# Transfers begun on GpSimd's queue in a two-layer recurrent decoder step on one core

## The chip, the core and the metric

The kernel runs on one core of a Trainium2 chip. The time is that of one execution on the device, in microseconds; "before" is the median of three runs, 2912.96 us (2909.19 to 2916.35). One more execution was profiled; its times are those of the rows below.

## The reference, cut to what matters

One inference step of a trunk of two layers is computed for 256 prompt tokens (one sequence) and 8 samples of 4 tokens each, in float32, with 2048 features. The same weights serve both groups.

```python
# layer 0: one projection feeds gated DeltaNet (8 heads, 128x128 state) and RG-LRU (width 1024)
proj = x @ w_in_e                                    # conv inputs, z, gate, a_pre, b_pre
conv_out, conv_new = causal_conv(conv_in, conv_buf, w_conv, b_conv)      # width 4
g, beta = -exp(a_log) * softplus(a_pre + dt_bias), sigmoid(b_pre)
o, s_new = gated_delta_rule(q, k, v, g, beta, s_delta)   # S = exp(g) S (I - beta k k^T) + beta k v^T
h, h_last = rg_lru(xr, r_pre, i_pre, lam, h_lru)         # h = a h + sqrt(1 - a^2) (i x)
mix = concat([rms_norm(o) * silu(z), h * gelu(gate)]) @ w_out_e
# layer 1: mLSTM, 8 heads, dk 128, dv 256, running-max stabiliser
h, c, n, m = mlstm_chunked(q, k, v, ig, fg, c0, n0, m0)
mix = (rms_norm(h) * sigmoid(o_pre)) @ w_out_o
# every layer
h = layer_norm(alpha * x + mix)
h = layer_norm(alpha * h + square(relu(h @ w_up)) @ w_down)
x = h + sigmoid(h @ w_ple_gate) * (p[layer] @ w_ple)
```

The outputs are y for both groups and all new states: the last three inputs of the convolutions, the DeltaNet, LRU and mLSTM states.

## The kernel before, in words

All 288 tokens (256 + 32) lie along the free dimension, features along the partitions. Each weight matrix is cut into slabs of 128x8x128 float32, 512 KB each. A slab is loaded into `raw` (line 394) and split into two float32r parts: ScalarE writes `hi`, a rounded copy (line 294), VectorE writes `lo = raw - hi` (line 295). The activations are split in the same way (`ah`/`al` and `bh`/`bl`), and each 128x128x288 product is three matmuls, hi*hi, lo*hi and hi*lo (line 416), 24 a slab. `raw` has four buffers, and three slabs are kept ahead in the two mixers (six elsewhere).

The kernel runs load, mixer of layer 0, output projection, LayerNorm, MLP, LayerNorm, gate, and then the same for layer 1. In a mixer the heads' work is written as generators, which `tick` advances by one step after every twelve slab matmuls, so that the small matmuls of the heads stand between those of the projection. TensorE works strictly in the order thus laid down, as does every other engine and every queue; the order of each is chosen ahead of time by the framework (Tile), which also places all semaphores. It may put an instruction that needs nothing earlier ahead of others: the state loads of line 1010 stand on SyncE's queue long before the heads that use them.

What moves by DMA, by place in the code:

- `load`: x, parameters, constants, first slabs (SyncE).
- `conv` (lines 672 and 676), 32 times: the samples' earlier inputs into `cin`, the new ones out of it. `cin` has two buffers. ScalarE copies the projection into the rest of `cin` in between.
- `delta_gates` (lines 703 to 727): a row of resets comes in, the cumulated log decays `gc` go out to DRAM (`dgc`), and three small arrays go out (`dds`) and come back with the samples' rows on the partitions (`rs`). These are begun on ScalarE's queue.
- `delta_head` (line 857): `gcb`, one head's row of `dgc`, comes back broadcast over 128 partitions. GpSimd copies the samples' parts of k, q, v, z and `gcb` (lines 861 to 863). Line 935 stores the prompt's state.
- `delta_sample`: 16 loads of four samples' states, 256 KB each, in four buffers (line 1010), each followed by two GpSimd copies into a window `win` (line 1019) and eight small matmuls that read the state itself; then 16 loads again, an update on VectorE and a store (line 1074).
- `lru_block` (line 1111): the two 128x128 gate weights `wri`.
- `mlstm_gates` (lines 1219 to 1268): as in layer 0, with `dng`, `mds`, `mrs`, `dw`, `w` and `scB`; begun on ScalarE's queue.
- `mlstm_head`: `ngb` (line 1304), the prompt's new state (line 1380), the samples' states `cn`, 514 KB each, in three buffers (line 1394) and their stores (line 1413).
- `scratch` (line 527): the layer's `p`. `gate`: the output y.

Of the kernel before, what the change touches and what calls it, by code (L numbers as in the profile page):

```python
# [16 lines left out]
NP, NS = 256, 32  # L17
NT = NP + NS
# [200 lines left out]
class Trunk:  # L219
# [299 lines left out]
    def scratch(self, layer):  # L519
        sm = self.sm  # L520
        T = lambda n, s, d=F32: sm.tile([128, *s], d, name=n, bufs=1)
        self.Y, self.Z = T("Y", [16, NT]), T("Z", [16, NT])
        self.s1, self.s2 = T("s1", [NT]), T("s2", [NT])
        self.mu, self.var, self.rstd, self.lnw = T("mu", [NT]), T("var", [NT]), T("rstd", [NT]), T("lnw", [NT])
        self.php = T("ph", [2, NT], F32R), T("pl", [2, NT], F32R)
        raw = T("praw", [2, NT])
        self.nc.sync.dma_start(raw, self.t["p"][layer])
        self.split(*self.php, raw)
        self.layer = layer
        self.extra = self.ex  # L530
        self.cap = 6
# [135 lines left out]
    def conv(self, lp, acc, c):  # L667
        nc, p = self.nc, self.p
        w = lambda j: p[:, P_WCONV + 4 * c + j:P_WCONV + 4 * c + j + 1]
        x = self.cin[self.ncin % len(self.cin)]  # L670
        self.ncin += 1
        nc.sync.dma_start(x[:, S0:], self.t["sconv"][c])
        nc.scalar.copy(x[:, 3:S0], acc[:, :NP])
        nc.scalar.copy(x[:, S0:].rearrange("p (b t) -> p b t", t=7)[:, :, 3:7],
                       acc[:, NP:].rearrange("p (b t) -> p b t", t=4))
        nc.sync.dma_start(self.t["conv"][c], x[:, NP:])
        out = lp.tile([128, S0 + 56], F32, name="cv")
        o = out[:, :NW]
        self.act(o, x[:, 3:3 + NW], AF.Identity, bias=p[:, P_BCONV + c:P_BCONV + c + 1], scale=w(3))
        for j in range(3):  # L680
            self.stt(o, x[:, j:j + NW], w(j), o, ALU.mult, ALU.add)
        return out
# [14 lines left out]
    def delta_gates(self, acc, lp, T):  # L697
        nc, p, c = self.nc, self.p, self.c
        acc = yield from self.gate_rows(acc, T)
        rg = T(40)  # L700
        nc.vector.memset(rg, 0.0)
        x, sp, g, rst = T(), T(), T(), T()
        nc.scalar.dma_start(rst, self.t["rows"][:, 0])
        self.act(x, acc[0:8], AF.Identity, bias=p[0:8, P_DT:P_DT + 1])
        be = rg[32:40]
        self.act(be, acc[32:40], AF.Tanh, scale=0.5)
        self.ts(be, be, 1.0, ALU.add, 0.5, ALU.mult)
        l = self.log1p_exp_neg_abs(x, T)
        self.ts(sp, x, 0.0, ALU.max)
        self.stt(sp, l, 2.0, sp, ALU.mult, ALU.add)  # L710
        ea = lp.tile([8, 1], F32, name="ea")
        self.act(ea, p[0:8, P_AL:P_AL + 1], AF.Exp)
        self.ts(g, sp, ea, ALU.mult, -1.0, ALU.mult)
        gc = rg[0:8]
        nc.vector.tensor_tensor_scan(out=gc, data0=rst, data1=g, initial=0.0, op0=ALU.mult, op1=ALU.add)
        self.dgc = self.dr.tile([8, NT], F32, name="dgc")
        nc.scalar.dma_start(self.dgc, gc)

        gl = T()[:, :NS].rearrange("h (b t) -> h b t", t=4)
        gs = gc[:, NP:].rearrange("h (b t) -> h b t", t=4)  # L720
        nc.vector.tensor_copy(gl, gs[:, :, 3:4].to_broadcast([8, 8, 4]))
        ds = self.dr.tile([3, 8, 8, 4], F32, name="dds")
        for n, r in enumerate((gs, be[:, NP:].rearrange("h (b t) -> h b t", t=4), gl)):
            nc.scalar.dma_start(ds[n].rearrange("b h t -> h b t"), r)
        self.rs = lp.tile([128, 3, 2], F32, name="rs")
        for n in range(3):
            nc.scalar.dma_start(self.rs[:, n], ds[n].rearrange("(g b) h t -> (b h t) g", g=2))

        for _ in range(LATE):
            yield  # L730
        tp = self.pm([128, 2, 40])
        for ch in range(2):
            self.tr(tp[:, ch], rg[:, ch * 128:(ch + 1) * 128])
        tg = lp.tile([128, 2, 40], F32, name="tg")
        nc.vector.tensor_copy(tg, tp)
        gT, self.bT = tg[:, :, 0:8], tg[:, :, 32:40]
        K = lambda n: lp.tile([128, 2, 8], F32, name=n)
        self.ngT, self.egT, self.negT, self.wT, self.eglB = K("ngT"), K("egT"), K("negT"), K("wT"), K("eglB")
        self.ts(self.ngT, gT, -1.0, ALU.mult)
        self.act(self.egT, gT, AF.Exp)  # L740
        self.ts(self.negT, self.egT, -1.0, ALU.mult)
        yield
        pl = self.pm([128, 2, 8])
        self.mm(pl, c[:, C_LAST:C_LAST + 128], gT)
        self.act(self.eglB, pl, AF.Exp)
        self.tt(self.wT, pl, gT, ALU.subtract)
        self.act(self.wT, self.wT, AF.Exp)
# [105 lines left out]
    def delta_head(self, lp, h, kq, v, z, out):  # L853
        nc = self.nc
        yield
        gcb = lp.tile([128, NT], F32, name="gcb")
        nc.sync.dma_start(gcb, self.dgc[h:h + 1].to_broadcast([128, NT]))
        cp = nc.gpsimd.tensor_copy
        gs, zsm = (a[:, NP:].rearrange("p (b t) -> p b t", t=4) for a in (gcb, z))
        for i, s in enumerate((kq[:, 0], kq[:, 1], v)):  # L860
# [71 lines left out]
        self.mm(p2[:, 1], ksc[:, 1], y[:, 1])  # L932
        self.tt(o[:, 1], o[:, 1], p2[:, 0], ALU.add)
        self.stt(S[:, 1], S[:, 0], self.eglB[:, 1, h:h + 1], p2[:, 1], ALU.mult, ALU.add)
        nc.sync.dma_start(self.t["delta_p"][h], S[:, 1])
        self.sumsq(lp, mo[:, 1:2], o[:, 1])
        f = self.delta_f(lp, ssq, mo)
        for ch in range(2):
# [17 lines left out]
    def delta_sample(self, lp, win, out):  # L956
# [50 lines left out]

        def load(h, g):
            s = lp.tile([128, 4, 128], F32, name="S", bufs=4)
            nc.sync.dma_start(s, state(h, g))  # L1010
            return s

        for g in range(2):
# [39 lines left out]
        for g in range(2):  # L1053
# [11 lines left out]
            for h in range(8):  # L1065
                s = load(h, g)
                pu = self.pm([128, 4, 128])
                self.mm(pu, kh, y4)
                if h < 7:
                    kh = keys(h + 1)  # L1070
                for b in range(4):
                    self.stt(s[:, b], s[:, b], self.eglS[:, h, 4 * g + b:4 * g + b + 1], pu[:, b],
                             ALU.mult, ALU.add)
                nc.sync.dma_start(self.t["delta_s"][h, :, 4 * g:4 * g + 4], s)
                yield

    def lru_consts(self, lp):
# [29 lines left out]
    def lru_block(self, lp, n, xr, gates, out):  # L1107
        nc, p = self.nc, self.p
        T = lambda nm, w=NW, **k: lp.tile([128, S0 + 56], F32, name=nm, **k)[:, :w]
        w = lp.tile([128, 2, 128], F32, name="wri")  # L1110
        nc.sync.dma_start(w, self.t["wri"][n])
        for _ in range(2):
            yield
        x = xr[:, :NW]
# [39 lines left out]
    def layer0_mixer(self, x, n_out):  # L1154
        nc, tc, t = self.nc, self.tc, self.t
        with ExitStack() as ctx:
# [47 lines left out]
                gates[n] = self.gelu(lr, next(accs))  # L1204
            self.finish(heads)
            self.finish()
            nc.sync.dma_start(t["lru"], self.hl)
        return out


    def mlstm_gates(self, acc, lp, T):
# [4 lines left out]
        rm = T(72)  # L1216
        nc.vector.memset(rm, 0.0)
        ig, fg, ls, B, d1, g, m, rst, rmx, ng = (T() for _ in range(10))
        nc.scalar.dma_start(rst, self.t["rows"][:, 1])
        nc.scalar.dma_start(rmx, self.t["rows"][:, 2])  # L1220
        self.act(ig, acc[0:8], AF.Identity, bias=p[0:8, P_IG:P_IG + 1])
        nc.vector.tensor_copy(fg, acc[32:40])
        self.ts(fg, fg, p[0:8, P_FG:P_FG + 1], ALU.add)
# [14 lines left out]
        mo = lp.tile([8, 9], F32, name="mout")  # L1238
        nc.vector.tensor_copy(mo[:, 0:1], m[:, NP - 1:NP])
        nc.vector.tensor_copy(mo[:, 1:9], b4(m)[:, :, 3])  # L1240
        nc.scalar.dma_start(self.t["mm"], mo)
        self.ts(ng, g, -1.0, ALU.mult)
        self.dng = self.dr.tile([8, NT], F32, name="dng")
        nc.scalar.dma_start(self.dng, ng)

        mg, nm, wr = (bt(T()[:, :NS]) for _ in range(3))
        sc = T()[:, :8]
# [3 lines left out]
        self.tt(sc, m0, b4(g)[:, :, 3], ALU.subtract)  # L1251
        ds = self.dr.tile([3, 8, 8, 4], F32, name="mds")
        for n, r in enumerate((b4(a), mg, nm)):
            nc.scalar.dma_start(ds[n].rearrange("b h t -> h b t"), r)
        self.rs = lp.tile([128, 3, 2], F32, name="mrs")
        for n in range(3):
            nc.scalar.dma_start(self.rs[:, n], ds[n].rearrange("(g b) h t -> (b h t) g", g=2))
        dw = self.dr.tile([8, 8, 4], F32, name="dw")
        nc.scalar.dma_start(dw, wr)
        self.w4 = lp.tile([128, 8], F32, name="w4")  # L1260
        for q in range(4):
            nc.scalar.dma_start(self.w4[32 * q:32 * q + 32], dw.rearrange("h b t -> (b t) h"))
        self.act(self.w4, self.w4, AF.Exp)
        self.ts(self.w4, self.w4, DKS, ALU.mult)
        dsc = self.dr.tile([8, 8], F32, name="dsc")
        nc.scalar.dma_start(dsc, sc)
        self.scB = lp.tile([128, 8, 8], F32, name="scB")
        nc.scalar.dma_start(self.scB, dsc[None].to_broadcast([128, 8, 8]))
        self.act(self.scB, self.scB, AF.Exp)

        for _ in range(LATE):
# [29 lines left out]
    def mlstm_head(self, lp, h, kq, v, win):  # L1301
        nc, c = self.nc, self.c
        ngb = lp.tile([128, NT], F32, name="ngb", bufs=1)
        nc.sync.dma_start(ngb, self.dng[h:h + 1].to_broadcast([128, NT]))
        smp = lambda a: a[:, NP:].rearrange("p (b t) -> p b t", t=4)
        cp = nc.gpsimd.tensor_copy
        wn = win[h % 2]
# [69 lines left out]
            self.mm(pc, ksc[:, ch], vt[:, ch, 0:257], ch == 0, ch == 1)  # L1377
        so = lp.tile([128, 257], F32, name="cs", bufs=1)
        nc.scalar.copy(so, pc)
        nc.sync.dma_start(self.t["mc_p"][h], so)  # L1380
        yield
        pt = self.pm([128, 2, 2, 128])
        for i in range(2):
# [6 lines left out]
        for g in range(2):  # L1390
            yield
            cn = lp.tile([128, 4, 257], F32, name="cn", bufs=3)
            gs = slice(4 * g, 4 * g + 4)
            nc.sync.dma_start(cn, self.t["smlstm"][h, :, gs])
            pin = self.pm([128, 257])
            for b in range(4):
                self.mm(pin[32 * b:32 * b + 32], wn[:, 4 * g + b, 28 - 4 * h:60 - 4 * h], cn[:, b])
# [8 lines left out]
            for b in range(4):  # L1406
                if b % 2 == 0:
# [2 lines left out]
                self.mm(pu, k8[:, b], v2)  # L1410
                self.stt(cn[:, b], cn[:, b], self.scB[:, h, 4 * g + b:4 * g + b + 1], pu[:, 0:257],
                         ALU.mult, ALU.add)
            nc.sync.dma_start(self.t["mc_s"][h, :, gs], cn)

    def mlstm_sample(self, lp):
        nc, c = self.nc, self.c
# [135 lines left out]
```

## Time and profile before

| | |
|---|---|
| median of three runs | 2912.96 us |
| profiled execution | 2916.8 us, its span 2915.0 us |
| TensorE matmuls | 2888.7 us busy, 99% of the span |
| VectorE, ScalarE, GpSimd | 1732.1, 1318.7, 57.9 us busy |
| granted TensorE clock | 0.999 of full speed over the span |
| DMA | 487.15 MB, 167 GB/s |

Busy time is that of an engine's own instructions; issuing a transfer is shown as an instruction of a queue (SPq is SyncE's, ACTq ScalarE's) and not counted as busy. In a timeline the brackets give the engine's idle time before an instruction and what ended it. The chain of waits is followed back from the last instruction, from each piece to what released it.

### The profile page before, as it was taken

How to read it: one execution, taken by the hardware profiler on the slowest of the kernel's cores; microseconds unless marked ns; L12 is line 12 of the kernel's file. 1: busy time of each engine (PE TensorE's matmuls, PEld its weight loads, DVE VectorE, ACT ScalarE, POOL GpSimd, SP SyncE). 2: the span in 40 equal slices, each digit the busy share in tenths (PEclk: the TensorE clock that was granted, in tenths of full speed). 3: DMA queues.
4: the chain of work that ended last, by engine and by line, in shares of the span. 5: the costliest groups of instructions: out<-in, count | busy, mean ns of one | idle time of the engine just before them, and what ended most of it. 6: DMA issues, size and time to landing. Idle time of an engine off the chain costs nothing.

```text
span 2915.0 us, 52851 instructions
## 1 busy us (share of the span) xinstructions
PE 2888.7 (99%) x21728; PEld 2839.1 (97%) x21728; DVE 1732.1 (59%) x2872; ACT 1318.7 (45%) x2171; POOL 57.9 (2%) x197
## 2 busy tenths in 40 slices
PE   8999999999999999999999999999999999999999
PEld 7999889999999999999999999999999999999999
DVE  7787787754454454455766666567445445445574
ACT  5555676543343343443634444436334334334362
POOL 1000100000000000000000000000000000000000
PEclk9999999999999999999999999999999999999999
DMA  6444475455555555555446665554555554555543
GB/s 225 134 127 128 151 233 174 134 191 166 167 164 164 165 167 166 162 165 166 159 157 201 198 201 172 184 167 159 166 163 163 167 167 162 165 166 166 165 156 132
DMA packets 155298, 487.15 MB, mean 167 GB/s; under 512 B 28552, under 2 KB 35888, under 8 KB 155056
## 3 DMA queue, kind: packets, MB, share of 16 engines
q1 hardware_dynamic: 151632, 483.68, 51.6%
q8 instruction: 170, 2.79, 0.4%
q10 hardware_dynamic: 3424, 0.10, 0.1%
q14 instruction: 72, 0.59, 0.1%
HBM read 466.12 MB, written 17.58 MB: 166 GB/s over the span
## 4 chain that ended last, share of the span: by engine, by line
PE 91%; DVE 5%; ACT 2%; DMA 1%; issue 1%; SPq 0%; ACTq 0%; DVEq 0%
PE acc L416 86%; PE m L268 4%; DVE Y L255 1%; DVE lo L295 1%; PE m L272 1%; ACT hi L294 1%; ACT junk L265 0%; PE m L470 0%; ACT L265 0%; DMA bh<-in_x 0%; DVE cv L258 0%; DVE al L255 0%; DVE mq L258 0%; DVE bl L255 0%; DMA S<-in_sdelta 0%
## 5 line engine op out<-in xcount | busy, mean ns | idle before, releaser
L295 DVE TENSOR_TENSOR lo<-raw,hi 128x1024 fp32r<-128x1024 f32 (+1 forms) x841 | 1027.1, 1223 | 680.6 <-ACT hi L294 679.6
L294 ACT CAST hi<-raw 128x1024 fp32r<-128x1024 f32 (+1 forms) x841 | 880.1, 1048 | 1007.3 <-PE acc L416 708.4
L416 PE MATMUL acc<-ah,hi 128*128 128x288 f32 x3328 | 998.9, 301 | 6.7 <-ACT hi L294 4.9
L416 PE MATMUL acc<-bh,hi 128*128 128x288 f32 x3328 | 989.6, 298 | 0.0
L416 PE MATMUL acc<-ah,lo 128*128 128x288 f32 x3328 | 985.1, 296 | 0.2 <-DVE lo L295 0.2
L416 PE MATMUL acc<-al,hi 128*128 128x288 f32 x3328 | 982.0, 297 | 0.9 <-DVE al L295 0.5
L416 PE MATMUL acc<-bh,lo 128*128 128x288 f32 x3328 | 981.3, 295 | 0.0
L416 PE MATMUL acc<-bl,hi 128*128 128x288 f32 x3328 | 974.1, 294 | 0.6 <-DVE bl L255 0.3
L416 PEld LDWEIGHTS acc<-ah,hi 128*128 128x128 f32 x3328 | 627.1, 189 | 12.6 <-ACT hi L294 4.9
L416 PEld LDWEIGHTS acc<-bh,hi 128*128 128x128 f32 x3328 | 624.0, 188 | 7.7 <-issue 7.1
L416 PEld LDWEIGHTS acc<-ah,lo 128*128 128x128 f32 x3328 | 627.7, 189 | 3.7 <-issue 2.3
L416 PEld LDWEIGHTS acc<-al,hi 128*128 128x128 f32 x3328 | 627.3, 189 | 3.6 <-issue 1.4
L416 PEld LDWEIGHTS acc<-bl,hi 128*128 128x128 f32 x3328 | 624.9, 188 | 1.8 <-DVE bl L255 0.8
L416 PEld LDWEIGHTS acc<-bh,lo 128*128 128x128 f32 x3328 | 625.2, 188 | 0.4
L265 ACT ACTIVATE tmp<-acc 128x288 f32<-128x288 f32 x160 | 65.8, 411 | 307.8 <-PE acc L416 307.7
L255 DVE TENSOR_TENSOR tmp<-tmp 128x288 f32<-128x288 f32 x128 | 58.8, 459 | 155.0 <-ACT tmp L265 155.0
L258 DVE SCALAR_TENSOR_TENSOR Y<-Y,acc 128x288 f32<-128x288 f32 x128 | 58.2, 455 | 112.0 <-PE acc L416 112.0
L258 DVE SCALAR_TENSOR_TENSOR cv<-cin,params,cv 128x312 f32<-128x312 f32 x96 | 51.5, 536 | 0.5
L258 DVE SCALAR_TENSOR_TENSOR cn<-cn,scB,m 128x257 f32<-128x257 f32 x64 | 27.9, 478 | 18.9 <-PE m L268 18.9
L265 ACT ACTIVATE Y<-Y,params 128x288 f32<-128x288 f32 x64 | 37.5, 633 | 0.3
L294 ACT CAST bh<-tmp 128x288 fp32r<-128x288 f32 x80 | 34.7, 434 | 6.2 <-DVE tmp L258 4.4
L258 DVE SCALAR_TENSOR_TENSOR tmp<-tmp,Z 128x288 f32<-128x288 f32 x32 | 14.6, 457 | 38.3 <-ACT tmp L265 38.3
(386 smaller groups left out, 1554.0 us busy)
## 6 DMA issues: line engine op xcount, KB each, us to landing
raw<-in_w_up SPq DMA_DIRECT2D x256, 512.0 KB
raw<-in_w_down SPq DMA_DIRECT2D x256, 512.0 KB
raw<-in_w_in_o SPq DMA_DIRECT2D x96, 512.0 KB
raw<-in_w_in_e SPq DMA_DIRECT2D x95, 512.0 KB
raw<-in_w_gate SPq DMA_DIRECT2D x64, 512.0 KB
raw<-in_w_out_e SPq DMA_DIRECT2D x32, 512.0 KB
raw<-in_w_out_o SPq DMA_DIRECT2D x32, 512.0 KB
cn<-in_smlstm SPq DMA_DIRECT2D x16, 514.0 KB
```

Source lines behind the costliest of these rows:

```text
L255: return self.nc.vector.tensor_tensor(out=out, in0=a, in1=b, op=op)
L258: self.nc.vector.scalar_tensor_tensor(out=out, in0=a, scalar=s, in1=b, op0=op0, op1=op1)
L265: return self.nc.scalar.activation(out, a, f, **k)
L268: self.nc.tensor.matmul(out, l, r, start=start, stop=stop)
L272: self.nc.tensor.transpose(out, a, self.ident[:n, :n])
L294: self.nc.scalar.copy(hi, src)
L295: self.nc.vector.tensor_sub(lo, src, hi.bitcast(F32))
L416: self.nc.tensor.matmul(acc, l[:, k], x[r](8 * kb + k), start=at == 0, stop=at == n - 1)
```

## The change

All transfers but the weight slabs, x, parameters, constants, and the last output y are begun on GpSimd's queue (`nc.gpsimd.dma_start`) instead of SyncE's (`nc.sync`) and ScalarE's (`nc.scalar`). Sources, destinations, buffers and the places in the program text stay as they are. Cut to one place of each kind:

```diff
-        self.nc.sync.dma_start(raw, self.t["p"][layer])
+        self.nc.gpsimd.dma_start(raw, self.t["p"][layer])
...
-        nc.sync.dma_start(x[:, S0:], self.t["sconv"][c])
+        nc.gpsimd.dma_start(x[:, S0:], self.t["sconv"][c])
...
-        nc.sync.dma_start(self.t["conv"][c], x[:, NP:])
+        nc.gpsimd.dma_start(self.t["conv"][c], x[:, NP:])
...
-        nc.scalar.dma_start(self.dgc, gc)
+        nc.gpsimd.dma_start(self.dgc, gc)
...
-            nc.scalar.dma_start(ds[n].rearrange("b h t -> h b t"), r)
+            nc.gpsimd.dma_start(ds[n].rearrange("b h t -> h b t"), r)
...
-            nc.scalar.dma_start(self.rs[:, n], ds[n].rearrange("(g b) h t -> (b h t) g", g=2))
+            nc.gpsimd.dma_start(self.rs[:, n], ds[n].rearrange("(g b) h t -> (b h t) g", g=2))
...
-        nc.sync.dma_start(gcb, self.dgc[h:h + 1].to_broadcast([128, NT]))
+        nc.gpsimd.dma_start(gcb, self.dgc[h:h + 1].to_broadcast([128, NT]))
...
-            nc.sync.dma_start(s, state(h, g))
+            nc.gpsimd.dma_start(s, state(h, g))
...
-                nc.sync.dma_start(self.t["delta_s"][h, :, 4 * g:4 * g + 4], s)
+                nc.gpsimd.dma_start(self.t["delta_s"][h, :, 4 * g:4 * g + 4], s)
...
-        nc.sync.dma_start(w, self.t["wri"][n])
+        nc.gpsimd.dma_start(w, self.t["wri"][n])
...
-            nc.scalar.dma_start(self.w4[32 * q:32 * q + 32], dw.rearrange("h b t -> (b t) h"))
+            nc.gpsimd.dma_start(self.w4[32 * q:32 * q + 32], dw.rearrange("h b t -> (b t) h"))
...
-        nc.sync.dma_start(ngb, self.dng[h:h + 1].to_broadcast([128, NT]))
+        nc.gpsimd.dma_start(ngb, self.dng[h:h + 1].to_broadcast([128, NT]))
...
-            nc.sync.dma_start(cn, self.t["smlstm"][h, :, gs])
+            nc.gpsimd.dma_start(cn, self.t["smlstm"][h, :, gs])
...
-            nc.sync.dma_start(self.t["mc_s"][h, :, gs], cn)
+            nc.gpsimd.dma_start(self.t["mc_s"][h, :, gs], cn)
```

The other lines are alike: `rows` (resets of the scans), `delta_p`, `lru`, `mm`, `dng`, `mds`, `mrs`, `dw`, `dsc`, `scB` and `mc_p`. In all 212 transfers of an execution change their queue, 187 from SyncE's and 25 from ScalarE's.

## Rows read from the trace of the kernel before

**Rows 1.** The page: span; busy us, share and instructions of each engine.
```profile
span 2915.0 us, 52851 instructions
...
PE 2888.7 (99%) x21728; PEld 2839.1 (97%) x21728; DVE 1732.1 (59%) x2872; ACT 1318.7 (45%) x2171; POOL 57.9 (2%) x197
```

**Rows 2.** Busy time by stretch; each begins with its limits and length.
```profile
core 0: us, PE busy (x) PEld busy (x) DVE busy (x) ACT busy (x) POOL busy (x), PEclk, DMA share, GB/s
0.00:12.40 12.40, 4.98 (x15) 3.53 (x15) 4.74 (x10) 6.12 (x8) 1.20 (x8) 1.00 0.82 287
48.00:75.00 27.00, 23.73 (x167) 23.17 (x166) 21.95 (x60) 12.77 (x40) 7.45 (x9) 0.94 0.62 168
340.00:356.00 16.00, 14.94 (x219) 12.15 (x217) 11.80 (x27) 10.85 (x25) 6.36 (x20) 1.00 0.67 220
...
1512.00:1552.00 40.00, 37.31 (x269) 34.93 (x268) 29.96 (x69) 17.86 (x44) 4.04 (x15) 1.00 0.48 148
1552.00:1790.00 238.00, 238.00 (x1798) 226.93 (x1797) 151.30 (x315) 110.80 (x229) 15.02 (x68) 1.00 0.64 201
```

**Rows 3.** TensorE's timeline: start, length, instruction, idle time before it and releaser.
```profile
68.19 0.30 PE L268 MATMUL m<-t,cm 128*128 128x32 f32 x1 [3.27 <-DVE t L791]
...
345.99 0.32 PE L268 MATMUL m<-S,win 128*32 128x128 f32 x4 [1.06 <-DMA S<-in_sdelta]
...
1538.33 0.49 PE L268 MATMUL m<-vt,sT 128*128 128x257 f32 x1 [1.45 <-DVE sT L258]
```

**Rows 4.** Busy time by stretch, in the 2 us behind the first stall.
```profile
70.00:72.00 2.00, 2.00 (x10) 2.00 (x10) 2.00 (x6) 1.71 (x3) 0.00 (x0) 0.50 0.49 107
```

**Rows 5.** The chain of waits in order of time: start, length, what.
```profile
2.93 6.82 DMA bh<-in_x
...
48.55 3.36 DMA dds<-bl
51.92 4.61 DMA rs<-dds
...
1529.22 3.86 DMA dw<-al
1533.48 2.64 DMA w<-dw
```

**Rows 6.** The issues of the state loads: ns min/median/max, first and last start.
```profile
L1010 SPq DMA_DIRECT2D S<-in_sdelta x32: 327/354/814, 33.7 to 419.6; - x32
```

**Rows 7.** GpSimd's timeline: its first copy, and its longest instruction.
```profile
36.08 1.51 POOL L862 COPY zs<-z 128x32 f32<-128x32 f32 x1 [34.35 <-DVE z L258]
...
48.63 5.01 POOL L861 COPY ks<-kq 128x32 f32<-128x32 f32 x1 [3.28 <-DVE kq L258]
```

**Rows 8.** ScalarE's timeline: issues of transfers in the gates.
```profile
48.55 0.68 ACTq L724 DMA_DIRECT2D dds<-bl  x2
...
51.92 0.91 ACTq L727 DMA_DIRECT2D rs<-dds  x2
...
1533.10 2.46 ACTq L1262 DMA_DIRECT2D w<-dw  x4
```

**Rows 9.** SyncE's timeline: the first state load, and four at the sample states.
```profile
33.73 0.42 SPq L1010 DMA_DIRECT2D S<-in_sdelta  x1
...
340.56 2.83 SPq L1010 DMA_DIRECT2D S<-in_sdelta  x4
```

**Rows 10.** DMA issues in 340 to 426 us: count and size of each.
```profile
S<-in_sdelta SPq DMA_DIRECT2D x28, 256.0 KB
out_delta_s<-S SPq DMA_DIRECT2D x15, 256.0 KB
wri<-in_wri SPq DMA_DIRECT2D x5, 128.0 KB
```

**Rows 11.** DMA in the first 14 us.
```profile
DMA packets 1437, 4.22 MB, mean 301 GB/s; under 512 B 160, under 2 KB 269, under 8 KB 1437
```

**Rows 12.** The page's groups: VectorE's slab subtraction, busy us and mean ns.
```profile
L295 DVE TENSOR_TENSOR lo<-raw,hi 128x1024 fp32r<-128x1024 f32 (+1 forms) x841 | 1027.1, 1223 | 680.6 <-ACT hi L294 679.6
```

More of the change, by code (lines that the diff above doesn't have):

```diff
@@ L702, in delta_gates @@
         x, sp, g, rst = T(), T(), T(), T()
-        nc.scalar.dma_start(rst, self.t["rows"][:, 0])
+        nc.gpsimd.dma_start(rst, self.t["rows"][:, 0])
         self.act(x, acc[0:8], AF.Identity, bias=p[0:8, P_DT:P_DT + 1])
@@ L934, in delta_head @@
         self.stt(S[:, 1], S[:, 0], self.eglB[:, 1, h:h + 1], p2[:, 1], ALU.mult, ALU.add)
-        nc.sync.dma_start(self.t["delta_p"][h], S[:, 1])
+        nc.gpsimd.dma_start(self.t["delta_p"][h], S[:, 1])
         self.sumsq(lp, mo[:, 1:2], o[:, 1])
@@ L1206, in layer0_mixer @@
             self.finish()
-            nc.sync.dma_start(t["lru"], self.hl)
+            nc.gpsimd.dma_start(t["lru"], self.hl)
         return out
@@ L1218, in mlstm_gates @@
         ig, fg, ls, B, d1, g, m, rst, rmx, ng = (T() for _ in range(10))
-        nc.scalar.dma_start(rst, self.t["rows"][:, 1])
-        nc.scalar.dma_start(rmx, self.t["rows"][:, 2])
+        nc.gpsimd.dma_start(rst, self.t["rows"][:, 1])
+        nc.gpsimd.dma_start(rmx, self.t["rows"][:, 2])
         self.act(ig, acc[0:8], AF.Identity, bias=p[0:8, P_IG:P_IG + 1])
@@ L1240, in mlstm_gates @@
         nc.vector.tensor_copy(mo[:, 1:9], b4(m)[:, :, 3])
-        nc.scalar.dma_start(self.t["mm"], mo)
+        nc.gpsimd.dma_start(self.t["mm"], mo)
         self.ts(ng, g, -1.0, ALU.mult)
         self.dng = self.dr.tile([8, NT], F32, name="dng")
-        nc.scalar.dma_start(self.dng, ng)
+        nc.gpsimd.dma_start(self.dng, ng)
         mg, nm, wr = (bt(T()[:, :NS]) for _ in range(3))
@@ L1253, in mlstm_gates @@
         for n, r in enumerate((b4(a), mg, nm)):
-            nc.scalar.dma_start(ds[n].rearrange("b h t -> h b t"), r)
+            nc.gpsimd.dma_start(ds[n].rearrange("b h t -> h b t"), r)
         self.rs = lp.tile([128, 3, 2], F32, name="mrs")
         for n in range(3):
-            nc.scalar.dma_start(self.rs[:, n], ds[n].rearrange("(g b) h t -> (b h t) g", g=2))
+            nc.gpsimd.dma_start(self.rs[:, n], ds[n].rearrange("(g b) h t -> (b h t) g", g=2))
         dw = self.dr.tile([8, 8, 4], F32, name="dw")
-        nc.scalar.dma_start(dw, wr)
+        nc.gpsimd.dma_start(dw, wr)
         self.w4 = lp.tile([128, 8], F32, name="w4")
         for q in range(4):
-            nc.scalar.dma_start(self.w4[32 * q:32 * q + 32], dw.rearrange("h b t -> (b t) h"))
+            nc.gpsimd.dma_start(self.w4[32 * q:32 * q + 32], dw.rearrange("h b t -> (b t) h"))
         self.act(self.w4, self.w4, AF.Exp)
@@ L1265, in mlstm_gates @@
         dsc = self.dr.tile([8, 8], F32, name="dsc")
-        nc.scalar.dma_start(dsc, sc)
+        nc.gpsimd.dma_start(dsc, sc)
         self.scB = lp.tile([128, 8, 8], F32, name="scB")
-        nc.scalar.dma_start(self.scB, dsc[None].to_broadcast([128, 8, 8]))
+        nc.gpsimd.dma_start(self.scB, dsc[None].to_broadcast([128, 8, 8]))
         self.act(self.scB, self.scB, AF.Exp)
@@ L1379, in mlstm_head @@
         nc.scalar.copy(so, pc)
-        nc.sync.dma_start(self.t["mc_p"][h], so)
+        nc.gpsimd.dma_start(self.t["mc_p"][h], so)
         yield
```

## The prediction

> **What bounds the kernel now.** I read the page's busy times first. TensorE's matmuls cover 2888.7 of the 2915.0 us span [rows 1], so the only time that a change of queues can win or lose is TensorE's idle time, 26.3 us now, and the time it spends below its full clock. The stretches come next, since an average over the span hides where that idle time sits [rows 2]. The start, 0 to 12.4 us, holds 7.4 us of it. The window with layer 0's gates, 48 to 75 us, holds 3.27; the one with the sample states, 340 to 356 us, 1.06; the one with layer 1's gates, 1512 to 1552 us, 2.69. The heads of layer 1, 1552 to 1790 us, hold none at all, though they carry 514 KB state loads. Then TensorE's own timeline: three instructions show what ended a wait [rows 3]. At 68.19 it had waited 3.27 us for VectorE's `t` of the first head, at 345.99 it had waited 1.06 us for a state load itself, at 1538.33 it had waited 1.45 us for VectorE's `sT`. The first stall costs twice: right behind it, in 70 to 72 us, the granted clock is 0.50, the lower of its two levels (1.2 and 2.4 GHz), and ten matmuls fill the 2 us [rows 4]. Over the 27 us stretch the clock averages 0.94, so some 0.06 x 27 = 1.6 us were lost on top of the 3.27; the two shorter stalls left the clock at 1.00 in their stretches [rows 2].
>
> The chain of waits says what stood behind these stalls [rows 5]: 3.36 us for the write of `dds` to DRAM and 4.61 us for `rs` coming back, 3.86 and 2.64 us for `dw` and `w`, and 6.82 us for x at the start. All but the last are transfers that this change moves.
>
> **The change part by part.** 212 transfers move to the queue of GpSimd, 187 from SyncE's and 25 from ScalarE's. The slabs, x and constants stay, and so do the bytes; only the issuer, the order behind which each waits, and the cost of issuing change.
>
> *The price of one issue.* No transfer begins on GpSimd in the trace of before. The same state load took SyncE's queue 0.327 us at least and 0.814 at most [rows 6]; the longest instruction that GpSimd itself shows is a copy of 128x32 that took 5.01 us beside a busy VectorE [rows 7]. These are the ends; I take 0.81 us, the upper figure of the same transfer, since GpSimd's ordinary instruction, 57.9 us over 197 = 0.29 us [rows 1], shows that it is not slow in itself. 212 x 0.81 = 172 us, in a queue that is busy for 58 now: it has room on average, so only places matter.
>
> *What is removed.* ScalarE no longer issues, nor waits in its queue for `dds` and `dw` to land (four loads of `w` alone held it 2.46 us [rows 8]); SyncE's slab issues no longer stand behind waiting stores. The second earns nothing where TensorE has no idle time. The first earns at most the three stalls that transfers end: 3.27 + 1.6 of clock, 1.06 and 1.45, together 7.4 us. But the data that ScalarE and VectorE wait for must still make the same two trips through DRAM.
>
> *The start.* GpSimd's queue has nothing between its memsets and a first copy at 36.08 us [rows 7], while SyncE's first state load came at 33.73 us, behind slabs [rows 9], 300 us before its use. On an empty queue whatever needs no earlier work goes at once: one row of constants, two conv states, one `wri`, four state loads, 1.25 MB from the sizes [rows 10]. The first 14 us move 4.22 MB at 301 GB/s [rows 11], and x is on the chain for 6.82 us of them [rows 5]. 1.25 MB / 301 GB/s = 4.1 us if all of it lands ahead of x, 0 if the framework, which orders each queue in advance, keeps them back. Issued 0.81 us apart from 1.7 us on, about half lands too late to matter: I take 2.1.
>
> *Gates of layer 0.* `dgc` and two writes of `dds`, then two loads of `rs`, must be issued one behind the other. ScalarE's queue needed 0.68 us for two writes, 0.34 each, and 0.91 for the two loads [rows 8]. Three at 0.81 are 2.4 instead of 1.0, two are 1.6 instead of 0.9, so `rs` lands 2.1 us later; the copy of 5.01 us at 48.63 [rows 7] is ready at the same moment, and if it stands ahead, 7.1. Both ends are kept, and below them -4.9, if ScalarE's conversions now go ahead of the wait. I take 2.1, since most copies take far less. Behind ScalarE's wait stand its slab conversions, behind them VectorE, 21.95 of 27 us busy there [rows 2].
>
> *Gates of layer 1.* Once the scans are done fourteen issues follow each other: `mm`, `dng`, two of `mds`, three of `mrs`, `dw`, `dsc`, four of `w`, `scB`. With one `mrs` ahead of it `dw` is the sixth: 6 x (0.81 - 0.34) = 2.8 us later. The four loads of `w` take 3.2 instead of 2.46 [rows 8]. So `w` lands 3.6 us later, and `ngb`, which shares the queue now, about as much; TensorE's slack was used up at 1538.33 [rows 3]. Taken: 3.6; ends -2.7 (that window's idle time gone) and 11.3 (fourteen times 0.81, none of it beside anything).
>
> *Sample states.* 28 of the 32 state loads fall into 340 to 426 us, with 15 stores and 14 smaller transfers, `wri` the largest of them [rows 10]. At 340.56 four loads were issued in 2.83 us [rows 9]. On GpSimd they share the queue with the two `win` copies of each head: 4 x 0.81 + 8 x 0.29 = 5.6 us, 2.8 later, on a wait that already held TensorE 1.06 us [rows 3]. Later loads show no wait of TensorE, so I count this once; ends -1.06 and 15, five such groups.
>
> *Clock.* With these terms the waits at 346 and 1538 grow to 3.9 and 5.1 us, past the 3.27 us that was followed by the lower level; 2 x 1.6 = 3.2 us.
>
> *The rest*, conv states in and out, `gcb`, `delta_p`, `wri`, `cn`, `mc_s`, `mc_p`, `praw`, `lru`: 0. The cover is the time between issue and use; the full TensorE in layer 1's heads [rows 2] shows it for the largest of them. If it is gone in places, up to 10 us.
>
> Sum: 2.1 + 2.1 + 3.6 + 2.8 + 3.2 = 13.8 us. The profiled execution took 2916.8 us, 1.8 of it outside its span, and would take 2930.6; it lies 3.84 us over the median of the runs, 2912.96, so the forecast for the median is 2926.8.
>
> **A rule that speaks against the change.** The long copy [rows 7] stands beside VectorE working nearly without a break [rows 2]: something of VectorE's delays GpSimd. The Trainium skill, "SBUF — State Buffer", section "Who interferes with whom", says that a transfer begun by GpSimd can stall while VectorE runs an instruction that takes both of their shared ports, because the descriptors cannot be written then. No run here shows a transfer so held. What it would do here is the third rival below.
>
> **Rivals.** *Cover holds (no change).* The framework orders every queue by its own estimate of each transfer, and will put the users later. Then the gates cost what they cost now and only part of the start is paid: 0 to 6 us, 2915. For it: 238 us without idle time in layer 1. Against it: three stalls exist already, at round trips the framework also planned.
>
> *Freed ScalarE (faster).* Its places are 51.92 us, where ScalarE's queue issues `rs`, and 1529 us, where it waits for `dw` [rows 5]. If its conversions go on while GpSimd waits, VectorE's chain starts earlier, and the stalls of 3.27, 1.06 and 1.45 us with the 1.6 of clock go: 2912.96 - 7.4 = 2905.6. It decides when `rs` and `w` are wanted later than 7 us after their gates. Against it: the first head needs `gcb`, which makes the same trip.
>
> *GpSimd is the bound in the sample states.* If each of the 57 transfers in 340 to 426 us also waits for one of VectorE's slab subtractions, 1.223 us [rows 12], the queue needs 57 x (0.81 + 1.22) = 116 us in 86, and state loads come 30 us late: 2943. For it: the copy of 5.01 us; against it: GpSimd's mean of 0.29 us. This is the way that the rule of the skill would take.
>
> **How the numbers follow.** Forecast 0.48 (its own range 2916 to 2940), cover 0.30, freed ScalarE 0.10, GpSimd the bound 0.12. 0.3%, about what can be told from no change, is 8.7 us: 2904.2 to 2921.7 is no change. The forecast lies above it in about 0.40 of its 0.48; with the 0.12 of the bound, slower has 0.52. Freed ScalarE at 2905.6 is faster in somewhat over half of its 0.10, 0.06; the rest, 0.42, is no change. The range, 2907 to 2955, leaves the faster end and sums in which several upper bounds meet.
>
> **What would show it.** TensorE's first wait for x ends later than 12.4 us, with four state loads landing in that time; the wait ended by `t` near 68 us and that by `sT` near 1538 us grow, with the clock at 0.50 behind them; the first wait for `S` near 346 us is 3 to 4 us. GpSimd's issues last about 0.8 us. TensorE's idle time outside these places stays as it is. Issues of 0.3 us or of 2 us would make the sum wrong, and so would state loads that don't go first; slower heads in layer 1 would show that the cover I counted at nothing is not there.

## The result and the profile after

The changed kernel takes 2942.2 us (median of 4 runs, 2941.26 to 2943.25) against 2914.01 us of the kernel before, timed beside it: a ratio of 1.0099, 95% interval 1.0081 to 1.0116, or 28.2 us more. The profiled execution took 2943.25 us, its span is 2941.5, 26.5 us longer than in [rows 1]. One execution of conv_sync below took 7228.2 us at a granted clock of 0.482; the times given for that kernel are those of its three others.

The page of the changed kernel (busy us, share, instructions):

```profile
span 2941.5 us, 52909 instructions
...
PE 2898.6 (99%) x21728; PEld 2846.7 (97%) x21728; DVE 1734.1 (59%) x2872; ACT 1319.8 (45%) x2171; POOL 172.3 (6%) x409
```

TensorE does the same 21728 matmuls in 9.9 us more, at a granted clock of 0.995 over the span against 0.999 before, and its idle time is 42.9 us instead of 26.3 [rows 1]: 16.6 more. Together these are the 26.5. GpSimd has 212 instructions more, the issues, which count as busy on this engine, and 114.4 us more busy time, 0.54 each. It is idle for 94% of the span, and in the sample states, 340 to 426 us, for 50.8 of 86 us, so the loss isn't work that GpSimd couldn't get through.

Its stretches, with the columns of [rows 2]; layer 1 begins 22 us later than before, so its gates stand in 1545 to 1580 here:

```profile
0.00:12.40 12.40, 6.24 (x18) 4.59 (x19) 5.15 (x10) 6.01 (x7) 5.55 (x16) 1.00 0.84 295
48.00:75.00 27.00, 19.34 (x133) 18.78 (x132) 17.43 (x51) 11.65 (x36) 10.81 (x19) 0.87 0.47 144
340.00:356.00 16.00, 15.42 (x170) 13.14 (x168) 12.56 (x35) 10.37 (x23) 6.93 (x16) 1.00 0.48 153
356.00:382.00 26.00, 23.77 (x291) 20.61 (x292) 15.75 (x40) 15.31 (x34) 14.64 (x39) 0.93 0.62 209
405.00:425.00 20.00, 17.40 (x91) 13.55 (x91) 15.01 (x44) 13.16 (x23) 7.73 (x16) 0.91 0.62 205
1545.00:1580.00 35.00, 29.80 (x202) 27.70 (x202) 20.84 (x56) 16.23 (x40) 14.01 (x31) 0.90 0.45 125
1580.00:1790.00 210.00, 210.00 (x1586) 200.32 (x1585) 130.65 (x266) 96.69 (x198) 35.47 (x102) 1.00 0.64 206
```

The start lost nothing, and the heads of layer 1 behind their gates still have no idle time. The gates of layer 0, the sample states and the gates of layer 1 each lost TensorE time, and each lost clock on top. In the kernel before, 356 to 382 and 405 to 425 us held 0.25 and 0.19 us of idle time at a clock of 1.00. TensorE's timeline names what ended its waits, as [rows 3] did before:

```profile
71.56 1.06 PE L268 MATMUL m<-t,cm 128*128 128x32 f32 x4 [7.66 <-DVE t L791]
...
92.09 0.66 PE L268 MATMUL m<-t,cm 128*128 128x64 f32 x4 [1.81 <-ACT t L265]
...
358.23 1.05 PE L268 MATMUL m<-S,win 128*32 128x128 f32 x16 [2.72 <-DMA S<-in_sdelta]
...
418.51 1.10 PE L268 MATMUL m<-y,kh 128*128 128x512 f32 x2 [2.44 <-DVE lah L255]
...
1561.87 0.48 PE L272 MATMUL m<-consts,v 128*128 128x128 f32 x1 [4.64 <-POOL v L1317]
```

The stall at the first head grew from 3.27 to 7.66 us. That at the first state load grew from 1.06 to 2.72. The one at layer 1's gates is a new one: it is ended by GpSimd's copy of `v`, not by `sT`.

For the experiments the spans are cut at three places that every trace has: the first gate product (line 470), the last copy of `yy` (line 909), and LayerNorm's first row. "Heads" lies between the first two, "states" (with the LRU and the output projection) between the second and third; "mixer 1" runs from layer 0's second LayerNorm, so with its gate, to layer 1's first. All in us, from one profiled execution each:

```
                  heads  states  mixer 1
before            322.0   217.5   586.5
after             333.8   229.1   590.5
gcb_sync          327.1   224.0   590.8
states_sync       336.3   216.8   592.7
stores_sync       333.5   223.4   590.8
gates1_back       330.8   227.9   586.5
gates0_back       331.9   224.3   590.2
four_back         317.5   218.0   590.6
five_back         317.8   220.3   586.8
```

The profiled execution of before lies 3.8 us over its median, so a difference of a few us in heads alone means little.

### The profile page after: what moved, and what is told of

It reads as the page before. It is cut to its first block, busy times and chain, and to the rows that moved or that the text cites. A ratio compares the mean times of both kernels' runs of the same rounds, so it can differ in the third digit from the quotient of the medians.

```text
span 2941.5 us, 52909 instructions
## 1 busy us (share of the span) xinstructions
PE 2898.6 (99%) x21728; PEld 2846.7 (97%) x21728; DVE 1734.1 (59%) x2872; ACT 1319.8 (45%) x2171; POOL 172.3 (6%) x409
## 4 chain that ended last, share of the span: by engine, by line
PE 88%; DVE 5%; issue 3%; DMA 2%; ACT 2%; POOL 1%; POOLq 0%; DVEq 0%; ACTq 0%
PE acc L416 84%; PE m L268 3%; DVE Y L255 1%; DVE lo L295 1%; DMA out_delta_s<-S 1%; PE m L272 1%; DMA gcb<-dgc 1%; ACT hi L294 0%; ACT junk L265 0%; DMA S<-in_sdelta 0%; ACT L265 0%; DVE cv L258 0%; POOL S L1010 0%; DVE al L255 0%; DVE bl L255 0%
```

## The experiments

Two theories stood at the start. Theory A: the loss is in the round trips and their places in GpSimd's queue, above all `gcb`. Rival: the framework orders the work differently when the queues differ, and that order costs the time. Each edit below is cut to one of its places; the amounts are differences of medians (before was 2911.5 to 2914.0 beside these kernels).

**gcb_sync**: the changed kernel with only `gcb` back.

```diff
-        nc.gpsimd.dma_start(gcb, self.dgc[h:h + 1].to_broadcast([128, NT]))
+        nc.sync.dma_start(gcb, self.dgc[h:h + 1].to_broadcast([128, NT]))
```

> The changed kernel with one kind of transfer back on SyncE's queue: the eight loads of gcb. Theory A (one queue in order: on GpSimd a load of gcb stands behind a store of cin that waits for ScalarE, and ScalarE then stands still for the load): ScalarE's waits for gcb fall from 17.1 us to about 4, the stalls of 1.8 and 2.3 us near 92 and 111 us and part of the 7.7 us near 71 us go, time 2942 to between 2930 and 2935. Rival B (the framework's changed order of TensorE's and VectorE's work makes the loss; that order stays here, since TensorE's order is the same as in the changed kernel): 2939 to 2943. Rival C (transfers begun on GpSimd take longer to land): like A here, told apart by gcb_only.

Measured: 2930.55 us (ratio to before 1.0062, 1.0045 to 1.0079), 11.7 us less than the changed kernel. The orders of TensorE and VectorE are the changed kernel's, so those aren't what this cost. ScalarE's isn't: with `gcb` on GpSimd the first five `eglS`, the small copies that read `gcb`, stand 2 to 9 instructions earlier in ScalarE's order. So the rival isn't out for ScalarE, and no run here held that order fixed. What `gcb` does stands in ScalarE's timeline of the changed kernel:

```profile
57.22 0.22 ACT L265 ACTIVATE eglS<-gcb 128x8 f32<-128x8 f32 x1 [6.32 <-DMA gcb<-dgc]
...
90.05 0.21 ACT L265 ACTIVATE eglS<-gcb 128x8 f32<-128x8 f32 x1 [3.25 <-DMA gcb<-dgc]
110.45 0.21 ACT L265 ACTIVATE eglS<-gcb 128x8 f32<-128x8 f32 x1 [2.99 <-DMA gcb<-dgc]
```

ScalarE works in order too, so the conversions of the next slabs stand behind `eglS`, VectorE's `lo` behind them, and TensorE last. With `gcb` on SyncE no wait at these three places is ended by it; at the first, ScalarE stands 6.20 us for `rs` instead, which is still on GpSimd's queue, and at the two later ones it doesn't wait. TensorE's first stall only fell from 7.66 to 5.68 us. In the table, 6.7 us of the gain stand in the heads and 5.1 in the states, where no `gcb` is loaded; how the gain gets there isn't shown.

**gcb_bufs3** and **gcb_only**: the changed kernel with three buffers for `gcb`, and the kernel before with only `gcb` on GpSimd.

```diff
-        gcb = lp.tile([128, NT], F32, name="gcb")
+        gcb = lp.tile([128, NT], F32, name="gcb", bufs=3)
```

> The changed kernel with three buffers of gcb instead of two, so that a load may go one head earlier, still on GpSimd's queue. Theory A: the loads go ahead of the store of cin where a buffer lets them; ScalarE's waits for gcb fall well below 17.1 us, time 2930 to 2937. Rival B: 2939 to 2943. Rival C (slower landing): a head's time of about 35 us covers any landing, so as A.

> The kernel before with only the eight loads of gcb begun on GpSimd; no store of cin and no other transfer is on that queue. Theory A: only GpSimd's copies stand in front, time 2912 to 2917, ScalarE's waits for gcb near the 4.0 us of before. Rival C (slower landing by itself): ScalarE's waits for gcb as in the changed kernel, 15 us or more, time 2922 to 2926. Rival B: TensorE's order is that of before, so 2912 to 2915.

Measured: 2939.65 us (1.0092, 1.0077 to 1.0107) and 2920.67 us (1.0027, 1.0018 to 1.0036). A buffer more gives little (its four runs lie at 2937 and at 2942 to 2944), so it isn't the reuse of a buffer; `gcb` alone costs some 8 us, between what theory A and rival C had said.

**conv_sync**: the changed kernel with the 64 conv transfers back on SyncE. In the changed kernel the `gcb` of each of the two later waits stands right behind an `out_conv` that waits for ScalarE:

```profile
84.65 0.54 POOL L676 DMA_DIRECT2D out_conv<-cin  x1 [0.94 <-ACT cin L674]
85.18 0.54 POOL L857 DMA_DIRECT2D gcb<-dgc  x1
105.07 0.55 POOL L676 DMA_DIRECT2D out_conv<-cin  x1 [8.73 <-ACT cin L674]
105.61 0.54 POOL L857 DMA_DIRECT2D gcb<-dgc  x1
```

```diff
-        nc.gpsimd.dma_start(self.t["conv"][c], x[:, NP:])
+        nc.sync.dma_start(self.t["conv"][c], x[:, NP:])
```

> The changed kernel with the 64 transfers of the convolutions (loads of in_sconv, stores out_conv) back on SyncE's queue; gcb stays on GpSimd's. TensorE's order is that of the changed kernel. Theory A (gcb stands behind a store of cin that waits for ScalarE): ScalarE's waits for gcb fall from 17.1 us to 8 or less, time 2942 to between 2931 and 2937. Rival C (what costs is gcb's own trip when GpSimd begins it, behind GpSimd's copies, as gcb_only's 8 us suggest): the waits for gcb stay at 11 us or more, time 2939 to 2943.

Measured: 2936.21 us, the median of 2936.16, 2936.21 and 2941.42 (1.0087, 1.0070 to 1.0104), 6.0 us less than the changed kernel; the profiled execution is the slowest of the three. In it ScalarE still waits 15.2 us for `gcb`, 17.1 in the changed kernel. For `gcb` the neighbour in the queue looked guilty in the timeline and isn't: without it `gcb` waits on its own for the same engine at these two places. The conv transfers still cost something in this company, by the three runs 1 to 6 us; where isn't shown.

**copy_act** and **gcb_copy_act**: the first `gcb` stood behind the slow copy of [rows 7]. Here the copies of k and q go to ScalarE, without and with `gcb` on GpSimd.

```diff
-            cp(self.ks[:, i, :, :, h], self.perm(self.smp(s)))
+            (nc.scalar.copy if i < 2 else cp)(self.ks[:, i, :, :, h], self.perm(self.smp(s)))
```

> A control: the kernel before, in which only the copies of k and q into ks (line 861, two a head) go from GpSimd to ScalarE; no transfer is moved. Both theories: the time of before within 3 us (2909 to 2915), since sixteen copies of some 0.2 us are added to ScalarE, which is 45% busy, and GpSimd's copies held up nothing that TensorE waited for. More than 4 us slower would mean that ScalarE has no room at the first heads, and the run beside it has to be read against this one.

> The kernel before with gcb's eight loads on GpSimd (which alone cost 8.3 us) and the copies of k and q into ks on ScalarE. Theory A (gcb stands behind the slow copy of k and q, 5.02 us in the run with gcb alone, in GpSimd's ordered queue): gcb of the first head is issued under 4 us after dgc instead of 5.7, TensorE's first stall goes from 6.58 back towards 3.3 us, and the loss against the copies' control falls to 0 to 4 us. Theory B (the trip itself costs more when GpSimd begins it, whatever is ahead): the loss against the control stays at 6 to 9 us and ScalarE's wait at eglS stays near 5.9 us.

Measured: 2913.06 us (0.9998, 0.9989 to 1.0007) and 2920.36 us (1.0028, 1.0018 to 1.0039), a loss of 7.3 against the control, as the rival had it. But GpSimd's timeline in gcb_copy_act shows why this run didn't test what it was meant to:

```profile
49.21 4.41 POOL L1019 COPY win<-ks 128x16 f32<-128x16 f32 x1 [4.28 <-ACT ks L861]
53.57 1.20 POOL L857 DMA_DIRECT2D gcb<-dgc  x2
```

The next copy, half as large and 0.2 us long elsewhere, took the place of the first one and lasted 4.41 us, to 53.62. VectorE's timeline in the same place:

```profile
51.95 1.20 DVE L295 TENSOR_TENSOR lo<-raw,hi 128x1024 fp32r<-128x1024 f32 x1
53.08 0.46 DVE L258 SCALAR_TENSOR_TENSOR kq<-silu,cv 128x312 f32<-128x312 f32 x1
53.47 0.17 DVE L262 TENSOR_SCALAR ngT<-tg 128x16 f32<-128x16 f32 x1
```

VectorE worked from before 46 us on without a pause, mostly on large instructions with two inputs in SBUF like the first two of these; the last of them ended at 53.54. In the kernel before, the copy of k ended at 53.64 and such an instruction at 53.56; in gcb_only at 51.65 and 51.57, in the changed kernel at 51.73 and 51.63. Behind it VectorE paused in before and gcb_only, and in the other two it went on with small instructions, so a pause isn't needed.

**free_copies** and **gcb_free**: those `win` copies (first group, first two heads) go to ScalarE as well, so nothing stands ahead of the first `gcb`.

```diff
-                    nc.gpsimd.tensor_copy(wn[:, i, :, 28:32], ks[:, i, g, :, h])
+                    (nc.scalar.copy if g == 0 and h < 2 else nc.gpsimd.tensor_copy)(wn[:, i, :, 28:32], ks[:, i, g, :, h])
```

> A control: the kernel before, in which GpSimd's copies of k and q into ks (line 861) and the win copies of the first two heads' first group (line 1019) go to ScalarE; no transfer is moved. Both theories: within 3 us of before (2909 to 2916).

> The control free_copies with gcb's eight loads on GpSimd. Theory A (any GpSimd copy ahead of gcb is held until VectorE pauses, and gcb with it): no copy stands ahead of the first gcb now, it is issued under 4 us after dgc (5.8 with the win copy ahead), and the loss against the control falls from 7.7 to 1 to 5 us. Theory B (the trip costs more by itself when GpSimd begins it): gcb is issued as early, but the loss stays at 6 to 9 us. If the issue itself takes over 2 us beside VectorE, issuing is held as copies are.

Measured: 2913.63 us (1.0004, 0.9995 to 1.0013) and 2917.51 us (1.0018, 1.0009 to 1.0028): the loss falls from 7.3 to 3.9 us (by the scatter of the runs the fall is 1 to 6). GpSimd's timeline, and then VectorE's in the same place, in gcb_free:

```profile
50.62 1.20 POOL L857 DMA_DIRECT2D gcb<-dgc  x2 [5.74 <-DMA dgc<-bl]
```

```profile
50.16 1.21 DVE L295 TENSOR_TENSOR lo<-raw,hi 128x1024 fp32r<-128x1024 f32 x1
51.29 0.52 DVE L258 SCALAR_TENSOR_TENSOR cv<-cin,params,cv 128x312 f32<-128x312 f32 x1
```

The wait before the issue is now ended by `dgc` itself, and two issues go through in 0.60 us each while VectorE is busy. So theory A holds for about half: a GpSimd copy is held while VectorE runs a series of such instructions, a transfer's issue isn't, and behind a held copy every transfer of the queue waits. Which of VectorE's instructions hold it was not tried. The other 3.9 us go with more waits of ScalarE at `eglS` (9.6 us in 7 of them, 2.6 in 3 for the control); TensorE's waits don't show them, the two profiled executions being 2915.93 and 2917.23 us. Their cause stays open, and the rival is one of the candidates: TensorE's and VectorE's orders are the control's, but the second head's `eglS` is ScalarE's 48th instruction instead of its 72nd. ScalarE's timelines, of gcb_free and then of the control:

```profile
54.78 0.22 ACT L265 ACTIVATE eglS<-gcb 128x8 f32<-128x8 f32 x1 [2.10 <-DMA gcb<-dgc]
57.37 0.22 ACT L265 ACTIVATE eglS<-gcb 128x8 f32<-128x8 f32 x1 [2.37 <-DMA gcb<-dgc]
...
57.59 1.03 ACT L294 CAST hi<-raw 128x1024 fp32r<-128x1024 f32 x1
```

```profile
55.12 1.04 ACT L294 CAST hi<-raw 128x1024 fp32r<-128x1024 f32 x1
...
62.06 0.21 ACT L265 ACTIVATE eglS<-gcb 128x8 f32<-128x8 f32 x1
```

The framework put both small copies, and with them the waits, ahead of a slab's conversion.

**states_sync**, **states_only**, **stores_sync**: state loads and stores back on SyncE; these alone on GpSimd in the kernel before; only the stores back.

```diff
-                nc.gpsimd.dma_start(self.t["delta_s"][h, :, 4 * g:4 * g + 4], s)
+                nc.sync.dma_start(self.t["delta_s"][h, :, 4 * g:4 * g + 4], s)
```

> The changed kernel with the 32 loads of S and the 16 stores of delta_s back on SyncE's queue. From the trace of the changed kernel 11.7 us are lost between the first use of S and the LayerNorm. Theory A (loads and stores of the states hold up each other and conv's and wri's transfers in one queue with GpSimd's copies): time 2942 to between 2929 and 2934, TensorE's wait for S near 1 us, VectorE's waits for S from 9.6 to about 3 us. Rival B (another order of the work): 2938 to 2943.

> The kernel before with only the 32 loads of S and 16 stores of delta_s begun on GpSimd. Theory A, in its strict form (only the company of the other transfers on that queue does the harm): 2912 to 2916. Rival C (the states' chain of load, update and store is itself slower when GpSimd begins it, and waits for GpSimd's copies): the 7.8 us that states_sync gave back, so 2918 to 2922, with VectorE's waits for S well above the 3.2 us of before.

> The changed kernel with only the sixteen stores delta_s back on SyncE; the state loads stay on GpSimd. Theory A (second half of the sample states: a load that waits for an earlier store to land stands in front of the next store in the same queue): most of the 7.8 us that taking back loads and stores together gave, 4 to 8 us, and VectorE's waits for S in the second half gone. Theory B (the loss is in the first half, where loads share GpSimd's queue with the win copies and wri): 0 to 2 us, with TensorE's wait for S near 358 us still 2.7 us.

Measured: 2934.38 us (1.0072, 1.0057 to 1.0087), 7.8 less than the changed kernel, with the states stretch back at 216.8; 2920.57 us (1.0030, 1.0018 to 1.0042), 9.1 over the 2911.45 of before beside it, as rival C had it; and 2937.51 us (1.0086, 1.0071 to 1.0101), 4.7 less. So the stores carry more than half of it. GpSimd's timeline in the changed kernel:

```profile
419.88 0.54 POOL L1010 DMA_DIRECT2D S<-in_sdelta  x1 [3.70 <-DMA out_delta_s<-S]
420.41 0.55 POOL L1074 DMA_DIRECT2D out_delta_s<-S  x1
421.01 0.54 POOL L1010 DMA_DIRECT2D S<-in_sdelta  x1
...
426.10 0.54 POOL L1010 DMA_DIRECT2D S<-in_sdelta  x1 [4.42 <-DMA out_delta_s<-S]
426.62 1.08 POOL L1074 DMA_DIRECT2D out_delta_s<-S  x2
```

A load needs a buffer, so it waits for an earlier store to land, and the next stores, ready or not, are issued right behind it: each round pays a landing. The wait row of that tile adds it up:

```profile
  DMA out_delta_s<-S: 21.2, 8
```

With the stores on SyncE the same row says 10.6 us in 4 waits.

**gates1_back** and **gates0_back**: the transfers of one layer's gates (with `ngb` in layer 1) back where they were.

```diff
-            nc.gpsimd.dma_start(self.w4[32 * q:32 * q + 32], dw.rearrange("h b t -> (b t) h"))
+            nc.scalar.dma_start(self.w4[32 * q:32 * q + 32], dw.rearrange("h b t -> (b t) h"))
```

> The changed kernel with the transfers of layer 1's gates back on ScalarE's queue and ngb back on SyncE's. From the trace of the changed kernel 4.0 us are lost between layer 1's gate products and its LayerNorm. Theory A (fourteen issues of 0.55 to 0.75 us in a row, with GpSimd's copies of v waiting behind them): the 4.6 us stall of TensorE for GpSimd's copy v goes, one of 1 to 2 us for sT comes back, time 2942 to between 2936 and 2939. Rival B (another order of the work): 2940 to 2943 and the loss between these two marks stays at 4.

> The changed kernel with the nine transfers of layer 0's gates back on ScalarE. The forecast's term says 2.1 us and its share of the clock, 1.6: 2 to 5 us faster than the changed kernel. The rival, that gcb's lateness hides this term, since ScalarE waits for gcb at the same place anyway: 0 to 1.5 us.

Measured: 2936.96 us (1.0083, 1.0068 to 1.0098), 5.2 less, with mixer 1 fully back; 2936.73 us (1.0078, 1.0063 to 1.0093), 5.5 less. For layer 1 the changed kernel's GpSimd timeline shows the reason:

```profile
1557.28 0.58 POOL L1304 DMA_DIRECT2D ngb<-dng  x1
1558.34 2.33 POOL L1262 DMA_DIRECT2D w<-dw  x4 [0.48 <-DMA dw<-al]
1560.66 0.57 POOL L1268 DMA_DIRECT2D scB<-dsc  x1
...
1561.52 0.29 POOL L1317 COPY v<-mv 128x128 f32<-128x128 f32 x1
```

The copy of `v` is GpSimd's own work, wanted by TensorE, and stands behind the whole train of issues. For layer 0 the 5.5 us can't be placed: TensorE's first stall is no shorter (7.96 us), and most of the gain stands in the states, where none of these transfers is. ScalarE stood 8.55 us for `gcb` there, as it stood 6.20 for `rs` in gcb_sync, so either transfer alone keeps this stall; with both back, in four_back, it is 0.94 us. In both gates runs the framework also ordered TensorE's, VectorE's and ScalarE's work differently than in the changed kernel, which wasn't separated.

**gcb_states_sync**, **four_back**, **five_back**: places taken back together. The first has `gcb` and the states on SyncE; four_back both layers' gates as well; five_back also `cn`, `mc_s` and `mc_p`.

```diff
-            nc.gpsimd.dma_start(cn, self.t["smlstm"][h, :, gs])
+            nc.sync.dma_start(cn, self.t["smlstm"][h, :, gs])
```

> The changed kernel with gcb, S and delta_s all back on SyncE's queue. If the two losses are separate they add: 2942.2 - 11.7 - 7.8 = 2922.7, between 2920 and 2925. If both are one (a queue that is late as a whole), it is what the better of them gave, 2929 to 2931. What is left over 2912.4 belongs to the gates' trips and the rest.

> The changed kernel with four things back where they were: gcb, the state loads and stores, and the transfers of both layers' gates with ngb. What stays on GpSimd: conv states, delta_p, wri, cn, mc_s, mc_p, p and the LRU state, 100 transfers in all. Theory A (the loss has three or four places and they add up): the time of before within 4 us, 2909 to 2917. Theory B (conv transfers on a queue of their own, or what the issues do to VectorE, cost something too): 2918 to 2923, with a TensorE idle time of over 30 us.

> The kernel four_back with layer 1's state loads and stores (cn, mc_s) and mc_p also back on SyncE; conv states, delta_p, wri, p and the LRU state stay on GpSimd. Theory A (the last loss is cn's load waiting for a store ahead of the copies that TensorE needs): layer 1's mixer is back at 586.5 us, TensorE's wait for vt at line 1326 (1.86 us) is gone, 2909 to 2915. Theory B (conv transfers cost it): 2915 to 2919, no change from four_back.

Measured: 2924.91 us (1.0043, 1.0029 to 1.0057), 2917.35 us (1.0019, 1.0010 to 1.0029), 2913.24 us (1.0003, 0.9993 to 1.0012). The last is the time of before, with the conv states, `delta_p`, `wri`, `p` and the LRU state still on GpSimd: those cost nothing that can be measured there. Nor does the order cost anything in it, though TensorE's differs from that of before in 35 places. In four_back, mixer 1 was still 4 us longer than before although its gates were back. GpSimd's timeline there:

```profile
1725.56 0.53 POOL L1394 DMA_DIRECT2D cn<-in_smlstm  x1 [5.13 <-DMA out_mc_s<-cn]
1726.09 0.60 POOL L1311 COPY vsr<-mv 128x32 f32<-128x32 f32 x1
1726.63 0.29 POOL L1317 COPY v<-mv 128x128 f32<-128x128 f32 x1
1726.86 0.10 POOL L1326 MEMSET vt<- 128x4 f32 x1
```

A load waits for a store to land, and copies that TensorE needs stand behind it; TensorE's next matmul at 1726.98 had waited 1.86 us. In five_back no such wait is left. In the changed kernel itself it doesn't show, 210 of 210 us being full there, so it depends on what comes before. No version beat the kernel before.

## Why the prediction was right or wrong

The direction was right, and 2942.2 us lies in the range; the forecast of 2926.8 was 15 us low. The step that failed is "**The rest**, conv states in and out, `gcb`, ...: 0. The cover is the time between issue and use". For `gcb` there was hardly any cover: it can go only when `dgc` has landed, ScalarE waited 4.0 us for it in the kernel before, and in the changed kernel 17.1. Taking it back gave 11.7 us; alone it cost 8.3, about half of that through the held copy, the rest by a cause that stays open. The layer whose full TensorE was taken as evidence for the cover holds no `gcb`. For the conv states, `wri`, `delta_p`, `p` and the LRU state the 0 was right in five_back, where the others are back; beside them the conv transfers cost some us (conv_sync). `cn`, `mc_s` and `mc_p` cost 4.1 in four_back, so the 0 was wrong there too. That 2942.2 lies in the range is in part luck: for the rest the prediction allowed at most 10 us, and `gcb` by itself gave more.

Step by step:

- *Issue price*, 0.81 us: 0.54, within the bounds and the same for 32 state loads; four loads of `w` took 2.33, no more than on ScalarE's queue [rows 8].
- *Start*, 2.1: nothing. Four state loads did go first, at 3.96 us, but gate products began at 21.7 us against 23.0 before.
- *Gates of layer 0*, 2.1: 5.5 when taken back alone. The stall by `t` near 68 us did grow and the clock behind it fell, as forecast, but not by `rs` alone: ScalarE's wait ended with `gcb` at 57.2 us, and `rs`, wanted next, landed at 57.6. Counted from the first gate product, `rs` was 2.4 us later than before, near the 2.1. The slow copy of [rows 7] did stand ahead, of `gcb` too, but took 3.38 us here and ran mostly beside the trip of `dds` to DRAM, so the end of 7.1, "if it stands ahead", didn't come.
- *Gates of layer 1*, 3.6 and 1.6 of clock: 5.2, right in size, in part by luck. The mechanism was half right: the delay is the train of issues, but it hits TensorE through GpSimd's own copy of `v`, which the prediction didn't count among what waits behind them.
- *Sample states*, 2.8 and 1.6 of clock: 7.8. The first wait for `S` grew to 2.72 us, near the 3 to 4 forecast. "Later loads show no wait of TensorE, so I count this once" failed: stores and loads on one queue delay each other, and 405 to 425 us holds 2.60 us of idle time at a clock of 0.91.
- *Clock*: 0.87, 0.93, 0.91 and 0.90 in four stretches instead of two falls; 9.9 us of busy time in all against 3.2 forecast. The single amounts above hold their share of it.

The single amounts (11.7, 7.8, 5.2, 5.5) add up to 30.2, and the four together gave 24.9: they overlap. What remained went with `cn`, `mc_s` and `mc_p`.

*Rivals.* The third, GpSimd the bound in the sample states, named 2943, nearly the measured time, and is wrong: the issues took 0.54 us beside VectorE, and GpSimd was idle in most of that stretch, waiting. Its 30 us were to stand in one place; states lost 11.6, the rest is elsewhere. The rule of the Trainium skill behind it ("SBUF — State Buffer", "Who interferes with whom") speaks of descriptors that can't be written while VectorE runs an instruction that holds both shared ports. The trace doesn't show that: two issues took 0.60 us each beside an unbroken VectorE. Whether the slab subtraction, which the rival took, holds both ports isn't shown either, so the rule itself isn't tested. The same section says that a VectorE instruction with two inputs in SBUF contends with a GpSimd instruction that reads SBUF; there the trace agrees in kind, since most instructions beside the held copies have two inputs (`raw` and `hi`, `cin` and `cv`), and shows more, since a copy of 0.2 us was held over several of them in a row, 3.38 to 6.24 us in all, and the transfers behind it with it. *Cover holds* and *freed ScalarE* are out by the time alone; ScalarE, freed of its issues, stood 6.32 us at `eglS` instead.

## What to carry to other kernels

Before a transfer moves to another engine's queue, list what that engine does itself just ahead of it and just behind it: an in-order queue passes each wait on in both directions. A round trip through DRAM whose result is wanted at once has no cover, whatever share of the queue is idle; count it by itself and never under "the rest". When a queue changes, look also at where the framework now puts the instruction that waits for the transfer: here it moved forward, ahead of work that was ready. A load that waits for a buffer should not share its queue with the stores that free the buffers, nor with copies that the bottleneck needs.

## What was not expected of the hardware

- GpSimd needed 0.54 us for an issue, 0.58 to 0.76 for those that scatter (`w`, `mrs`), beside a busy VectorE or not. From issue to landing `gcb` took 3.8 us (median) in the changed kernel, and 3.0 begun on SyncE in gcb_sync.
- GpSimd's small copies, 0.2 us as a rule, took 3.38, 4.41, 5.01 and 6.24 us in the same place of four kernels (after, gcb_copy_act, before, gates0_back), and each ended within 0.1 us of the end of a VectorE instruction with two inputs in SBUF, the last of a series.
